# Down projection of a gated MLP in seven block products instead of eight, with the block sums made beside the up projection

## The chip, the cores and the metric

The kernel runs on one core of one Trainium2 chip. The metric is the device time of one execution, in microseconds (us). The core has five engines that run side by side, each through its own list of instructions in order: TensorE (PE, matmuls; PEld is its weight load), VectorE (DVE), ScalarE (ACT), GpSimd (POOL), and SyncE (SP), which here issues all the DMAs. They wait for one another by semaphores. Matmuls write to PSUM, eight banks of 512 float32 for each of 128 partitions; everything else lies in SBUF or in device memory (DRAM).

## The reference, cut to what matters

One encoder layer on a sequence of 1024 positions with 1024 channels, batch 1, all in float32. A mixer of two groups of attention heads comes first and is not touched. The channel half is what the change works on:

```python
h = modulate(rmsnorm(x, g_mlp_norm[l]), sh_m, sc_m)
u = causal_dwconv(jnp.dot(h, w_up[l]), conv_w[l], conv_b[l])      # (1024, 5632)
gate, val = jnp.split(u, 2, axis=-1)
x = x + g_m[:, None, :] * jnp.dot(jax.nn.silu(gate) * val, w_down[l])  # w_down (2816, 1024)
```

`g_m` is a row of 1024 numbers, the last of six slices of `silu(c) @ w_ada + b_ada`; it multiplies the columns of the down product.

## The kernel before, in words

**Precision.** Every large product is made in three matmuls. An operand is split into a high half `hi` (the value as the type fp32r, made by ACT in `hi_of`) and a low half `lo` (the difference, made by POOL or DVE in `lo_of`, line 82), and the product is hi·hi + hi·lo + lo·hi, three matmuls of 128x128 by 128x512 into the same PSUM bank.

**Order.** The program is written with a tile framework. Tiles come from pools, a tag with `bufs=n` has n buffers in turn, and a new tile in a buffer waits for the readers of the old one. A scheduler with a timeline of its own sets the order of the instructions on each engine from the program; `tc.issue_after(x)` makes what is issued under it stand behind instruction x.

**Up phase.** `w_up` (1024 x 5632) is used in 22 tiles j, each with 128 gate and 128 value columns, over 1024 positions. The product of a 2 x 2 block weight (a11, a12, a21, a22, blocks of 512 x 128) with a 2 x 2 block activation is made in seven block products instead of eight, in the manner of Strassen and Winograd: seven sums of weight blocks times seven sums of activation blocks. The activation sums are made and split once ahead of the phase (pages `b11`, `b21`, `t3`, `t2`, `t1`, `t4`, `b22`). In each tile, `ff_head` loads two weight tiles `raw` and makes the products wa·b11 and wb·b21; `ff_tile` makes the weight sums on DVE (lines 1020 to 1035), splits them (ACT and POOL) and makes the products wc·t3, wd·t2, we·t1, wf·t4, wg·b22; each is 4 x 3 = 12 matmuls, so a tile has 84. The products are combined on DVE out of PSUM (lines 1026 to 1037) into c, four blocks of 512: gate and value for 1024 positions. `conv` makes the depthwise convolution (one ACT pass, line 1005, and two DVE passes, 1006 and 1007, for each of gate and value); SiLU (ACT, line 1041) and the product (DVE, line 1042) follow, and the result is stored to `g_d[j]` in DRAM, 128 x 1024.

**Gate row.** From tile 2 on, `gate_row` makes g_m in slices beside the tiles: it loads parts of `w_ada`, adds them up on DVE into `gmbc` (line 993, two passes of 512 in a tile, eight tiles), and two small matmuls bring the sum to all 128 partitions.

**Down phase** (lines 1054 to 1081). The positions are done in two halves h of 512. In each half, all eight PSUM banks hold sums for four position tiles t and two halves n of the output columns. For each of the 22 blocks j of 128 rows, a weight tile 128 x 1024 of `w_down` is loaded, multiplied by `gmbc` (DVE, line 1062) and split (ACT, and POOL for the low halves `wds`), 128 x 512 of `g_d` is loaded and split (ACT, DVE), and 24 matmuls follow (lines 1072 to 1074). Then DVE adds the residual x1 from DRAM (line 1080), and the rows are stored. The weights are loaded and split once in each half.

Of the kernel before, what the change touches and what calls it, by code (L numbers as in the profile page):

```python
# [62 lines left out]
def layer_kernel(ctx, tc, I, out):  # L63
# [3 lines left out]
    def f32(ap):  # L67
        return ap.bitcast(F32)
# [4 lines left out]
    def hi_of(eng, o, i):  # L73
        if eng == "a":
            act.activation(o, i, AF.Copy)  # L75
# [14 lines left out]
    g_d = dram.tile([NF, P, S], F32, name="g_d")  # L90
# [767 lines left out]
    B, v0, hpools = {}, {}, [h2p]  # L858
# [9 lines left out]
    def bpage(nm, k, v, le):  # L868
        pg = hpools[-1].tile([P, 2, 512], F32R, name=f"{nm}_{k}")
        hi_of("a", pg[:, 0], v[:])  # L870
        lo_of(le, pg[:, 1], v[:], pg[:, 0])
        B[nm, k] = pg
# [36 lines left out]
    hpools.append(bp2.__enter__())  # L909
# [15 lines left out]
    def product(pt, w, b):  # L925
        for k in range(4):
            sh, sl = w[:, 0, k * P:(k + 1) * P], w[:, 1, k * P:(k + 1) * P]
            pg = B[b, k]
            pe.matmul(pt, sh, pg[:, 0], start=(k == 0), stop=False)  # L929
            pe.matmul(pt, sh, pg[:, 1], start=False, stop=False)  # L930
            pe.matmul(pt, sl, pg[:, 0], start=False, stop=(k == 3))  # L931

    def ff_head(j, p1, p2):
# [6 lines left out]
        product(p1, split(raw[0][:, :512], f"wa{j}", "w2"), "b11")  # L940
        product(p2[:, :512], split(raw[0][:, 512:], f"wb{j}", "w2"), "b21")
        return raw, p1, p2

    pre = ps2.tile([P, 1024], F32, name="op_0", tag="op", bufs=3)
    head = ff_head(0, pre[:, :512], pre[:, 512:])
    pc = mt("raw", [P, D], "p12_0")
    act.activation(pc[:], pre[:], AF.Copy)
    head = (head[0], pc[:, :512], pc[:, 512:])
# [23 lines left out]
    def bank(tag, name, n=1):  # L972
        return ps3.tile([P, n * 512], F32, name=name, tag=tag, bufs=1)
# [36 lines left out]
    def ff_tile(j, head):  # L1010
        raw, p1, p2 = head
        a11, a12, a21, a22 = raw[0][:, :512], raw[0][:, 512:], raw[1][:, :512], raw[1][:, 512:]
        p5, p6, p34 = bank("p5", f"p5_{j}"), bank("p6", f"p6_{j}"), bank("p34", f"p34_{j}", 2)

        c = mt("c", [P, 7, 512], f"c{j}")
        if j:
            act.activation(c[:, 0], p1, AF.Copy)

        t3 = mt("s", [P, 512], f"ws3_{j}")
        dve.tensor_tensor(t3[:], a11, a21, op=SUB)  # L1020
        p7 = p2[:, 512:] if j else bank("p1", "p7_0")[:]
        product(p7, split(t3[:], f"wc{j}"), "t3")
        dve.tensor_tensor(a21, a21, a22, op=ADD)
        dve.tensor_tensor(a11, a21, a11, op=SUB)
        product(p6[:], split(a11, f"wd_{j}"), "t2")
        dve.tensor_tensor(c[:, 6], c[:, 0] if j else p1, p6[:], op=ADD)
        if j:
            dve.tensor_tensor(c[:, 0::5][:, 0:2], c[:, 0::6][:, 0:2], p2[:].rearrange("p (a b) -> p a b", a=2), op=ADD)
        else:
            dve.tensor_tensor(c[:, 0], p1, p2, op=ADD)  # L1030
            dve.tensor_tensor(c[:, 5], c[:, 6], p7, op=ADD)
        product(p5[:], split(a21, f"we{j}"), "t1")
        dve.tensor_tensor(c[:, 3:5], c[:, 5:7], p5[:].unsqueeze(1).to_broadcast([P, 2, 512]), op=ADD)
        product(p34[:, 512:], split(a22, f"wf{j}"), "t4")
        dve.tensor_tensor(a12, a12, a11, op=SUB)
        product(p34[:, :512], split(a12, f"wg{j}"), "b22")
        dve.tensor_tensor(c[:, 1:3], c[:, 4:6], p34[:].rearrange("p (a b) -> p a b", a=2), op=ADD)  # L1037
# [3 lines left out]
        act.activation(ug[:], ug[:], AF.Silu)  # L1041
        dve.tensor_tensor(ug[:], ug[:], uv[:], op=MUL)
        sp.dma_start(g_d[j], ug[:])

    gr_gen = gate_row()
    for j in range(NF):
        if j:
            head = ff_head(j, bank("p1", f"p1_{j}")[:], bank("p27", f"p27_{j}", 2)[:])
        ff_tile(j, head)
        if j >= 2:  # L1050
            next(gr_gen, None)


    for h in range(2):
        wide = [bank(n, f"dn{n}_{h}", 2) for n in ("p27", "p34")]
        pts = [[w[:, :512], w[:, 512:]] for w in wide]
        for x in (("p1", "p6"), ("p5", "G")):
            pts.append([bank(n, f"dn{n}_{h}")[:] for n in x])
        for j in range(NF):
            raw = mt("raw", [P, D], f"wd{h}_{j}")  # L1060
            sp.dma_start(raw[:], I["w_down"][j * P:(j + 1) * P, :])
            dve.tensor_tensor(raw[:], raw[:], gmbc[:], op=MUL)  # L1062
            w = [split(raw[:, n * 512:(n + 1) * 512], f"wds{h}_{j}{n}") for n in range(2)]
            gr = mt("s", [P, 512], f"gr{h}_{j}")
            sp.dma_start(gr[:], g_d[j][:, h * 512:(h + 1) * 512])
            g = mt("w2", [P, 2, 512], f"g{h}_{j}", F32R)
            hi_of("a", g[:, 0], gr[:])
            lo_of("v", g[:, 1], gr[:], g[:, 0])
            for t in range(4):
                sh, sl = g[:, 0, t * P:(t + 1) * P], g[:, 1, t * P:(t + 1) * P]  # L1070
                for n in range(2):
                    pe.matmul(pts[t][n], sh, w[n][:, 0], start=(j == 0), stop=False)  # L1072
                    pe.matmul(pts[t][n], sh, w[n][:, 1], start=False, stop=False)  # L1073
                    pe.matmul(pts[t][n], sl, w[n][:, 0], start=False, stop=(j == NF - 1))  # L1074
        for t in range(4):
            xt = mt("u", [P, D], f"xo{h}{t}")
            sp.dma_start(xt[:], x1_d[4 * h + t])
            for n in range(2):
                c = slice(n * 512, (n + 1) * 512)
                dve.tensor_tensor(xt[:, c], xt[:, c], pts[t][n], op=ADD)  # L1080
            sp.dma_start(out[(4 * h + t) * P:(4 * h + t + 1) * P, :], xt[:])
# [5 lines left out]
    hpl.__exit__(None, None, None)  # L1087
# [69 lines left out]
```

## Time and profile before

| | us |
|---|---|
| median of 3 runs (1454.95 to 1457.18) | 1456.5 |
| the profiled execution | 1456.2 |
| its span, first to last instruction | 1454.4 |
| PE busy in the span | 1270.4 (87%) |
| DVE busy | 1029.9 (71%) |
| POOL busy | 770.3 (53%) |
| ACT busy | 606.5 (42%) |
| first matmul of tile 0's wc in the up phase | at 770.0 |
| first matmul of the down phase | at 1194.4 |
| last matmul | at 1443.5 |
| granted TensorE clock, mean over the span | 0.936 |

How to read what follows: a row of the timeline is start, duration, engine, line, operation, output<-input, shape, count, and in brackets the idle time ahead of it on its engine with what ended it. A row of waits is the waiting engine and tile, who released it, the total, the number of times and the longest. A row of the groups has the count, then busy time and the mean in ns of one, then the idle time ahead of the group. Matmul durations overlap, since they are pipelined; the distance from one start to the next is what counts. DMA share is the mean busy share of the core's 16 DMA engines.

### The profile page before, as it was taken

Reading aid. Unit: us, or ns where it says so; the run is one execution under the profiler, and the core shown is the slowest. Engines: PE = TensorE matmul, PEld = TensorE weight load, DVE = VectorE, ACT = ScalarE, POOL = GpSimd, SP = SyncE. Lnnn points to the kernel's source line nnn. Section 1 sums busy time; section 2 is a strip of 40 time slices with the busy share of each in tenths; the row PEclk is TensorE's granted clock in tenths of the full one; section 3 lists DMA queues with packets and bytes.
Section 4 is the critical chain, followed back from the end, with each engine's and each line's share of the span. In section 5 each row is a group of like instructions: output and inputs, shape, how many; then the busy total and the mean of one; then the engine's idle time right before and its main releaser. Section 6 shows DMA issues by size and latency. Waiting matters only on the chain.

```text
span 1454.4 us, 20116 instructions
## 1 busy us (share of the span) xinstructions
PE 1270.4 (87%) x6836; PEld 1054.4 (72%) x6836; DVE 1029.9 (71%) x1838; ACT 606.5 (42%) x1182; POOL 770.3 (53%) x717
## 2 busy tenths in 40 slices
PE   3859988998877789886668999999999998999997
PEld 2749877887765568675546877888888887887885
DVE  6964776576688988782577778778777776566653
ACT  4544344334455555452374343443444433322331
POOL 5363544265545764333735655556655555665662
PEclk9979997999887799997878999999999999999999
DMA  7423547555522588778712322322222234447442
GB/s 283 135 70 77 130 107 144 133 119 118 114 59 55 107 162 171 149 145 261 243 41 87 116 88 101 107 82 87 88 87 87 96 130 152 152 142 241 146 145 101
DMA packets 214627, 183.85 MB, mean 126 GB/s; under 512 B 148214, under 2 KB 179066, under 8 KB 213500
## 3 DMA queue, kind: packets, MB, share of 16 engines
q1 hardware_dynamic: 214524, 182.56, 45.3%
q8 instruction: 54, 0.88, 0.3%
q14 instruction: 49, 0.40, 0.1%
HBM read 119.07 MB, written 28.84 MB: 102 GB/s over the span
## 4 chain that ended last, share of the span: by engine, by line
PE 23%; POOL 9%; DVE 8%; issue 8%; DMA 7%; ACT 1%; SPq 1%; DVEq 0%; POOLq 0%; ACTq 0%
PE p L929 5%; PE p L931 5%; PE p L930 5%; POOL wds L82 5%; DMA wu<-w_up 2%; PE dnp L1072 2%; PE dnp L1074 2%; PE dnp L1073 2%; DVE u L1007 1%; DMA wd<-w_down 1%; DVE ws L1020 1%; DVE u L1006 1%; POOL wf L82 1%; POOL we L82 1%; POOL wd L82 1%
## 5 line engine op out<-in xcount | busy, mean ns | idle before, releaser
L82 POOL TENSOR_TENSOR wds<-wd,wds 128x512 fp32r<-128x512 f32 x88 | 152.4, 1753 | 102.7 <-ACT wds L75 102.7
L82 POOL TENSOR_TENSOR wc<-ws,wc 128x512 fp32r<-128x512 f32 x22 | 65.2, 2962 | 136.7 <-ACT wc L75 136.7
L1062 DVE TENSOR_TENSOR wd<-wd,gmbc 128x1024 f32<-128x1024 f32 x44 | 68.5, 1556 | 84.1 <-DMA wd<-w_down 84.0
L1074 PE MATMUL dnp<-wds,g 128*128 128x512 f32 x308 | 119.3, 393 | 4.6 <-DVE g L82 4.6
L1072 PE MATMUL dnp<-wds,g 128*128 128x512 f32 x308 | 120.0, 392 | 1.8 <-DVE xo L1080 1.7
L75 ACT ACTIVATE wds<-wd 128x512 fp32r<-128x512 f32 x88 | 54.8, 624 | 159.1 <-PE dnp L1074 152.3
L1073 PE MATMUL dnp<-wds,g 128*128 128x512 f32 x308 | 120.1, 391 | 0.0
L71 POOL TENSOR_SCALAR hlm<-Pm,rim 128x512 f16<-128x512 f32 (+3 forms) x96 | 64.8, 685 | 78.9 <-DVE rim L684 39.7
L71 POOL TENSOR_SCALAR hlc<-Pc,ric 128x640 f16<-128x640 f32 (+2 forms) x64 | 46.2, 724 | 80.6 <-DVE ric L684 39.5
L1020 DVE TENSOR_TENSOR ws<-wu,wu 128x512 f32<-128x512 f32 x22 | 30.5, 1387 | 75.0 <-DMA wu<-w_up 75.0
L681 ACT ACTIVATE Pc<-sc,mc 128x640 f32<-128x640 f32 (+2 forms) x64 | 42.2, 660 | 91.0 <-DVE mc L670 64.1
L655 PE MATMUL sm<-mk,mq 96*128 96x512 f32 (+3 forms) x288 | 71.2, 377 | 10.2 <-ACT Pm L681 6.7
L1006 DVE SCALAR_TENSOR_TENSOR u<-c,pk,u 128x1023 f32<-128x1023 f32 x44 | 77.4, 1766 | 1.8 <-ACT u L1005 1.8
L1041 ACT ACTIVATE u<-u 128x1024 f32<-128x1024 f32 x22 | 23.4, 1063 | 132.1 <-DVE u L1007 132.1
L655 PE MATMUL sc<-k,q 64*128 64x512 f32 (+3 forms) x288 | 68.7, 365 | 10.7 <-ACT Pc L681 6.8
L82 DVE TENSOR_TENSOR g<-gr,g 128x512 fp32r<-128x512 f32 x44 | 69.8, 1588 | 11.2 <-ACT g L75 11.2
L430 DVE SCALAR_TENSOR_TENSOR aacc<-aw,cs,aacc 128x256 f32<-128x256 f32 x84 | 44.1, 525 | 47.3 <-DMA aw<-w_ada 47.0
L1005 ACT ACTIVATE u<-c,pk 128x1024 f32<-128x1024 f32 x44 | 52.3, 1236 | 56.1 <-DVE c L1037 56.1
L705 DVE SCALAR_TENSOR_TENSOR hlm<-Pm,rim,hlm 128x512 f16<-128x512 f32 (+3 forms) x96 | 68.5, 727 | 6.1 <-POOL hlm L71 5.9
L721 PE MATMUL pvm<-PTm,vt 128*128 128x128 f16 x576 | 47.2, 232 | 28.6 <-DMA PTm<-hlm 24.5
L1074 PEld LDWEIGHTS dnp<-wds,g 128*128 128x128 f32 x308 | 58.2, 189 | 18.0 <-DVE g L82 5.9
L1072 PEld LDWEIGHTS dnp<-wds,g 128*128 128x128 f32 x308 | 58.1, 189 | 15.1 <-DVE xo L1080 2.6
(366 smaller groups left out, 4281.1 us busy)
## 6 DMA issues: line engine op xcount, KB each, us to landing
wu<-w_up SPq DMA_DIRECT2D x44, 512.0 KB, 4.5
wd<-w_down SPq DMA_DIRECT2D x44, 512.0 KB, 5.1
aw<-w_ada SPq DMA_DIRECT2D x96, 128.0 KB, 2.4
g_d<-u SPq DMA_DIRECT2D x22, 512.0 KB, 2.6
gr<-g_d SPq DMA_DIRECT2D x44, 256.0 KB, 3.6
x<-x SPq DMA_DIRECT2D x16, 512.0 KB, 6.6
adaw<-w_ada_a SPq DMA_DIRECT2D x8, 1024.0 KB, 5.2
wq_r<-w_qk SPq DMA_DIRECT2D x32, 128.0 KB, 2.8
```

The source lines that it names most:

```text
L71: pool.tensor_scalar(o, i, s, 1.0, op0=MUL, op1=MUL)
L82: (pool if eng == "p" else dve).tensor_tensor(o, i, f32(hi), op=SUB)
L655: last = pe.matmul(s[:, c:c + w], qpg[rs_, a, q], kpgs[kh][rs_, b, ko:ko + w], start=(a == 0 and b == 0), stop=(a == 1))
L705: dve.scalar_tensor_tensor(hl[:, w:2 * w], pp, ri[:], hl[:, :w], op0=MUL, op1=SUB)
L929: pe.matmul(pt, sh, pg[:, 0], start=(k == 0), stop=False)
L930: pe.matmul(pt, sh, pg[:, 1], start=False, stop=False)
L931: pe.matmul(pt, sl, pg[:, 0], start=False, stop=(k == 3))
L1006: dve.scalar_tensor_tensor(u[:, 1:], c[:, :S - 1], pk[:, cv + 1:cv + 2], u[:, 1:], op0=MUL, op1=ADD)
L1062: dve.tensor_tensor(raw[:], raw[:], gmbc[:], op=MUL)
L1072: pe.matmul(pts[t][n], sh, w[n][:, 0], start=(j == 0), stop=False)
L1073: pe.matmul(pts[t][n], sh, w[n][:, 1], start=False, stop=False)
L1074: pe.matmul(pts[t][n], sl, w[n][:, 0], start=False, stop=(j == NF - 1))
```

## The change

The down product is now also made in seven block products. The 22 row blocks of `w_down` are taken in 11 pairs i (block 2i and 2i+1), the output columns in two halves, the positions in two halves, so that for each i there is a 2 x 2 block of weights (each 128 x 512) and a 2 x 2 block of activations (each 128 x 512). A stage is one of the seven products, summed over all 11 pairs in PSUM: 11 x 4 position tiles x 3 matmuls, in four banks. The stages P1, P2, P5, P6, P3, P7, P4 take two sets of four banks (A and B) in turn; P3 and P7 are added onto what P5 and P6 left in their banks.

- **Activation sums.** They are made on DVE in the up phase, at the end of a tile: one difference of 512 columns for even j, three sums for odd j. `g_d` now holds seven blocks for each pair, and `keep` stores them: 256 KiB twice for even j, 512 KiB twice and 256 KiB once for odd j. Down stages load one block of 256 KiB for each i.
- **Weight sums.** The four weight blocks of a pair are loaded once and stay in the tile `R[i]` (5 x 512; the fifth part is the activation). DVE makes the sums in place, in the stage before they are needed (`extra`).
- **Splits** in the down stages take weight and activation in one pass, 128 x 1024: ACT the high half, DVE the low half (`halves`); POOL has no part in the stages. The splits have four buffers, and a fifth now and then.
- **Early part.** In the last up tile, `early` loads and splits the first four pairs for stage P1.
- **Gate row at the output.** `gmbc` multiplies the output blocks instead of the weights. Output blocks are combined in SBUF (`p1s`, `w5`, `u2`), two position tiles at a time (128 x 1024), by items of `todo` put between the low halves from the sixth pair of a stage on; x1 is added to them. The last four blocks are multiplied, added and stored 512 columns at a time, and P4 does its last three pairs position tile by position tile (`group=3`).
- **Order.** `inorder` keeps DVE passes and SP loads of the stages in the program's order.
- **Up phase.** The PSUM tag p27 is gone: wb·b21 is added onto wa·b11 in the same bank, and ACT copies that bank twice. p1 has two banks, and `wa` and the weight sums of the next tile are issued ahead of `wg` of this one. Buffers: raw 4 for 3, s 7 for 5, u 3 for 2; c has 4 blocks for 7.

In PE's order the first product of tile 1 (wa·b11) stands ahead of tile 0's wc; before, nothing stood there. The diff, cut:

```diff
-    g_d = dram.tile([NF, P, S], F32, name="g_d")
+    g_d = dram.tile([7, NF // 2, P, 512], F32, name="g_d")
...
-    MB = {"raw": 3, "w2": 2, "s": 5, "ws": 5, "c": 2, "u": 2}
+    MB = {"raw": 4, "w2": 2, "s": 7, "ws": 5, "c": 2, "u": 3}
...
+    def halves(src, nm):
+        w = sptile(nm)
+        hi_of("a", w[:, 0], src)
+        if "dl" in E:
+            tt(w[:, 1], src, f32(w[:, 0]), SUB)
+        else:
+            lo_of("v", w[:, 1], src, w[:, 0])
+        return w
...
+    def early():
+        hpl.__exit__(None, None, None)
...
+        for i in range(4):
+            r = mt("raw", [P, D], f"de{i}").rearrange("p (a b) -> p a b", a=2)
+            sp.dma_start(r[:, 0], wsrc(i, 0))
+            sp.dma_start(r[:, 1], g_d[A_G11, i])
+            dq[i] = halves(r, f"dne{i}")
...
+        if j:
+            with tc.issue_after(p3_last[0]):
+                product(p1[:], wb, "b21", add=True)
+            act.activation(c[:, 0], p1[:], AF.Copy)
+            if j == NF - 1:
+                early()
...
+        product(p34[:, 512:], wf, "t4")
+        if j + 1 < NF:
+            raw, wa, wb = ff_load(j + 1)
+            q1 = bank("p1", f"p1_{j + 1}")
+            product(q1[:], wa, "b11")
+            d = mt("c", [P, 4, 512], f"c{j + 1}")
+            act.activation(d[:, 3], q1[:], AF.Copy)
+            nxt = ff_sums(j + 1, raw) + [wb, q1, d]
+        p3_last[0] = product(p34[:, :512], wg, "b22")
...
-        sp.dma_start(g_d[j], ug[:])
+        i = j // 2
+        lo, hi = ug[:, :512], ug[:, 512:]
+        sm = mt("s", [P, 512], f"gs{j}")
+        if j % 2 == 0:
+            us.append(ug)
+            keep(0, 1, i, lo)
+            dve.tensor_tensor(sm[:], lo, hi, op=SUB)
+            keep(6, 1, i, sm[:])
+        else:
+            ue = us.pop()
+            keep(1, 2, i, ug[:])
+            dve.tensor_tensor(ue[:, 512:], ue[:, 512:], hi, op=ADD)
+            dve.tensor_tensor(ue[:, :512], ue[:, 512:], ue[:, :512], op=SUB)
+            keep(3, 2, i, ue[:])
+            dve.tensor_tensor(sm[:], lo, ue[:, :512], op=SUB)
+            keep(5, 1, i, sm[:])
...
-            dve.tensor_tensor(raw[:], raw[:], gmbc[:], op=MUL)
-            w = [split(raw[:, n * 512:(n + 1) * 512], f"wds{h}_{j}{n}") for n in range(2)]
...
+    def stage(nm, bk, b, kind, add=False, wq=None, extra=None, todo=(), group=0):
...
+        for i in range(NK):
+            if wq is not None and not (nm == "P1" and i in dq):
+                wload(i, wq[0], wq[1])
+            if nm == "P2" and i in dq:
+                wload(i, 0, 0)
+            if nm == "P1" and i in dq:
+                w = dq[i]
+            else:
+                gload(i, kind)
+                w = halves(R[i][:, b::4 - b], f"dn{nm}_{i}")
+            if extra is not None:
+                extra(i)
+            if i < NK - group:
+                for t in range(4):
+                    mm3(bk, t, w, i == 0 and not add, i == NK - 1, add)
+            else:
+                held.append((i, w))
+            if i >= 5:
+                for _ in range(-(-len(todo) // (NK - i))):
+                    todo.pop(0)()
...
+    stage("P1", "A", 0, A_G11, wq=(0, 0))
+    stage("P2", "B", 1, A_G12, wq=(1, 2), todo=[copy_p1],
+          extra=lambda i: (wload(i, 2, 1), tt(R[i][:, 0], R[i][:, 2], R[i][:, 0], SUB)))
+    stage("P5", "A", 0, A_S1, todo=c11(),
+          extra=lambda i: (wload(i, 3, 3), tt(R[i][:, 0], R[i][:, 3], R[i][:, 0], SUB)))
+    stage("P6", "B", 0, A_S2, todo=[ext(wq_, p1s, "A", x) for x in range(2)],
+          extra=lambda i: tt(R[i][:, 2], R[i][:, 3], R[i][:, 2], SUB))
+    stage("P3", "A", 3, A_S4, add=True, todo=[ext(u2, p1s, "B", x) for x in range(2)],
+          extra=lambda i: tt(R[i][:, 1], R[i][:, 1], R[i][:, 0], SUB))
+    stage("P7", "B", 2, A_S3, add=True, todo=after(u2, u2, "A", 0, 1))
...
+    stage("P4", "A", 1, A_G22, todo=[ext(wq_, wq_, "B", 0), ext(wq_, wq_, "B", 1), ext(p1s, p1s, "B", 0), ext(p1s, p1s, "B", 1)]
+          + after(wq_, wq_, "B", 1, 1)[2:] + pre_, group=3)
+    for t in range(4):
+        o = dl.tile([P, 512], F32, name=f"oe{t}", tag="oe", bufs=3)
+        tt(o[:], banks[f"A{t // 2}"][:, t % 2], gmbc[:, :512], MUL)
+        tt(o[:], o[:], p1s[:, t], ADD)
+        sp.dma_start(out[(4 + t) * P:(5 + t) * P, :512], o[:])
```

More of the change, by code (lines that the diff above doesn't have):

```diff
@@ L923, in split, with product @@
         return w
-    def product(pt, w, b):
+    def product(pt, w, b, add=False):
         for k in range(4):
@@ L928, in product, with ff_load @@
             pg = B[b, k]
[L929 to L933, printed above, removed]
+            pe.matmul(pt, sh, pg[:, 0], start=(k == 0 and not add), stop=False, skip_group_check=add)
+            pe.matmul(pt, sh, pg[:, 1], start=False, stop=False, skip_group_check=add)
+            last = pe.matmul(pt, sl, pg[:, 0], start=False, stop=(k == 3), skip_group_check=add)
+        return last.ins
+    def ff_load(j):
         raw = []
@@ L1045, in layer_kernel @@
+        return nxt
     gr_gen = gate_row()
+    p3_last = [None]
+    cur = ff_sums(0, raw0) + [None, None, mt("c", [P, 4, 512], "c0")]
     for j in range(NF):
[L1047 to L1049 removed]
+        cur = ff_tile(j, cur)
         if j >= 2:
             next(gr_gen, None)
[L1054 to L1061, printed above, removed]
[L1062 to L1081 removed]
@@ new lines, in layer_kernel, with inorder, two @@
+    R[:3] = [dl.tile([P, 5, 512], F32, name=f"dnr{i}") for i in range(3)]
+    tail = {}
+    def inorder(eng, f, *a, **k):
+        if eng in tail:
+            with tc.issue_after(tail[eng]):
+                r = f(*a, **k)
+        else:
+            r = f(*a, **k)
+        tail[eng] = r.ins
+    banks = {}
+    for n in ("B0", "B1", "A0", "A1"):
+        banks[n] = None
+    def two(n, name):
+        banks[n] = ps4.tile([P, 2, 512], F32, name=name, tag=n, bufs=1)
+    for n in ("B0", "B1", "A0", "A1"):
+        two(n, f"dn{n}_0")
@@ new lines, in rows, with finish_out, mul, add @@
+    def rows(t0, n, d):
+        return d[t0:t0 + 2, :, n * 512:(n + 1) * 512].rearrange("t p c -> p t c")
+    out_v = out.rearrange("(t p) c -> t p c", p=P)
+    def finish_out(h, n, x, src, o, store=True):
+        t0 = 4 * h + 2 * x
+        xt = []
+        def mul():
+            xt.append(pair(f"xo{h}{n}{x}"))
+            load(xt[0][:], rows(t0, n, x1_d))
+            tt(o, src, gm_of(n), MUL)
+        def add():
+            tt(o, o, xt[0][:], ADD)
+            if store:
+                sp.dma_start(rows(t0, n, out_v), o)
+        return [mul, add]
```

156 lines of the change are left out of this document (122 added, 34 removed).

## The prediction

> **What bounds the kernel now.** I read the page first: span, engine shares, costliest groups.
>
> ```profile
> span 1454.4 us, 20116 instructions
> PE 1270.4 (87%) x6836; PEld 1054.4 (72%) x6836; DVE 1029.9 (71%) x1838; ACT 606.5 (42%) x1182; POOL 770.3 (53%) x717
> ```
>
> The profiled execution took 1456.2 us, 1.8 outside its span, and stands 0.3 below the median of 1456.5; sums below are against 1456.2. Then stages: a table of stretches (us; busy time of PE, PEld, DVE, ACT, POOL; granted clock; DMA share; GB/s). The first row is the up phase without gate-row work, the second with it, the third the down projection, the last two the densest loading.
>
> ```profile
> 1060.00:1155.00 95.00, 95.00 (x421) 78.65 (x420) 73.39 (x67) 40.06 (x55) 54.47 (x36) 1.00 0.25 84
> 866.75:946.65 79.90, 77.24 (x337) 62.77 (x337) 62.81 (x61) 31.16 (x44) 46.34 (x29) 1.00 0.30 106
> 1195.00:1444.00 249.00, 242.45 (x1055) 198.15 (x1053) 148.19 (x101) 77.25 (x129) 145.56 (x85) 0.99 0.46 152
> 0.00:20.00 20.00, 3.58 (x8) 1.45 (x8) 6.70 (x13) 11.48 (x21) 10.04 (x25) 1.00 0.90 340
> 1320.00:1340.00 20.00, 17.62 (x74) 13.30 (x73) 11.25 (x9) 5.23 (x9) 9.46 (x6) 1.00 0.83 288
> ```
>
> PE is never idle in the first row. Since a busy PE need not be PE at its peak, I took start to start from the timeline: the first matmul of two following tiles, the gap ahead of the first tile, a pair of slow starts after it, and the first and last matmul of the down projection.
>
> ```profile
> 1085.63 0.39 PE L929 MATMUL p<-t,wc 128*128 128x512 f32 x1
> 1104.67 0.39 PE L929 MATMUL p<-t,wc 128*128 128x512 f32 x1
> 770.04 0.80 PE L929 MATMUL p<-t,wc 128*128 128x512 f32 x1 [14.11 <-ACT wc L75]
> 773.10 0.63 PE L931 MATMUL p<-t,wc 128*128 128x512 f32 x1
> 773.52 0.63 PE L929 MATMUL p<-t,wc 128*128 128x512 f32 x1
> 1194.43 0.39 PE L1072 MATMUL dnp<-wds,g 128*128 128x512 f32 x1
> 1443.46 0.39 PE L1074 MATMUL dnG<-wds,g 128*128 128x512 f32 x1
> ```
>
> 84 matmuls in 19.04 us are 0.2267 us each, so both MLP phases are bound by their number of matmuls. The down projection has 2 halves x 22 x 4 x 2 x 3 = 1056; its 1055 steps need 239.1 us and took 249.0: 9.9 us are stalls. PE's waits, the first two rows in the up phase, the others in the down projection:
>
> ```profile
> PE p L929 <- ACT wc L75: 14.1, 1, 14.1
> PE p L929 <- DVE c L1028: 4.5, 6, 0.9
> PE dnp L1074 <- DVE g L82: 4.6, 3, 2.0
> PE dnp L1072 <- DVE xo L1080: 1.7, 2, 1.1
> ```
>
> The rest of the 9.9 are slow starts after such waits, like the 0.43 us step above.
>
> **The change, part by part.**
>
> *Matmuls.* Seven stages x 11 x 4 x 3 = 924 for 1056: 132 x 0.2267 = **-29.9 us**. The Trainium skill ("TensorE: Matmul & The Clock Gate", Back-to-back issue gap) gives N/2.4 + 2.5 ns for a lone matmul and about 131 ns sustained at N=512; by these the term would be 28.5 or 17.3 us (estimates from that page). The trace's 0.2267 us on fp32r fits neither, and decides.
>
> *Feeding the seven stages.* A step is 12 matmuls, 2.72 us. ACT makes one 128x1024 high half, DVE one low half; POOL does nothing. Rows for such passes, and spacings on DVE and POOL:
>
> ```profile
> L1041 ACT ACTIVATE u<-u 128x1024 f32<-128x1024 f32 x5 | 5.3, 1063 | 29.1 <-DVE u L1007 29.1
> L1005 ACT ACTIVATE u<-c,pk 128x1024 f32<-128x1024 f32 x10 | 11.9, 1236 | 3.6 <-DVE c L1037 3.6
> 1112.37 0.68 DVE L1024 TENSOR_TENSOR wu<-wu,wu 128x512 f32<-128x512 f32 x1
> 1112.98 1.21 DVE L1042 TENSOR_TENSOR u<-u,u 128x1024 f32<-128x1024 f32 x1
> 1114.11 0.68 DVE L1035 TENSOR_TENSOR wu<-wu 128x512 f32<-128x512 f32 x1
> 1114.71 0.67 DVE L1026 TENSOR_TENSOR c<-c,p 128x512 f32<-128x512 f32 x1
> 1115.42 1.22 DVE L1028 TENSOR_TENSOR c<-c,p 128x1024 f32<-128x1024 f32 x1
> 1113.01 2.94 POOL L82 TENSOR_TENSOR wc<-ws,wc 128x512 fp32r<-128x512 f32 x1 [5.83 <-ACT wc L75]
> 1115.90 1.30 POOL L82 TENSOR_TENSOR wd<-wu,wd 128x512 fp32r<-128x512 f32 x1
> 1117.16 1.30 POOL L82 TENSOR_TENSOR we<-wu,we 128x512 fp32r<-128x512 f32 x1
> ```
>
> ACT: 1.06 of 2.72, hidden. DVE: 1.21 for the low half, 0.68 for the weight-block sum that four stages (P2, P5, P6, P3) make for the next. The fullest stage is P5 with six 128x1024 output passes: 11 x 1.89 + 6 x 1.21 = 28.1 of 29.9 us. Hidden, but barely; the cover is four or five split buffers, about 8 us of lead. P4 has twelve output passes, two between each of its last low halves, and the first waits for P7's last matmul. Its sixth low half gets a buffer when the stage's second step ends (5.4), is done at 6.6, and five more rounds of 3 x 1.21 end at 24.8; the grouped last three blocks want it at 8 steps + 6 matmuls = 23.1. Cost between 0 and 5; I take **+2**.
>
> *The old stalls* come from the half change (xo) and the starved start (g); the new stages alternate two sets of four banks, so the next starts in banks read long before. **-9.9**, or 0 if as much returns. At the entry four blocks (10.9 us of PE) are split inside the last tile. Behind it DVE has one 1.22 add, then waits for ACT's first conv pass (1.24), has four conv passes of 1.2 and the first low half: about 9 us. Held, with 2 us to spare.
>
> *Loads.* 121 of 256 KiB, eight of x1, 4.2 MB out: 40 MB, 192 GB/s over the stages where the trace shows 152. P2 is the worst: 37 loads, 9.4 MB after the first, on SP behind the last tile's stores at about 16 us into the stages (three stores follow DVE's interleaved sums), due by 54.6: 243 GB/s. The rows with 340 and 288 show that the engines can; 0, up to +8 if not.
>
> *Tail.*
>
> ```profile
> 1447.70 1.28 DVE L1080 TENSOR_TENSOR xo<-xo,dnp 128x512 f32<-128x512 f32 x2 [5.25 <-DMA xo<-x_d]
> 1449.02 2.10 SPq L1081 DMA_DIRECT2D out_dram<-xo  x2
> 1450.07 0.68 DVE L1080 TENSOR_TENSOR xo<-xo,dnG 128x512 f32<-128x512 f32 x1
> ```
>
> Before, 10.9 us pass from the last matmul to the end: residual tiles wait for a buffer. After, x1 is added beforehand, and the last 512 columns take a multiply and an add: 0.4 + 2 x 0.68, then the store, 3.3 us as now (1451.1 to 1454.4): 5.1. **-5.8.** The gate row multiplied 44 weight tiles on DVE; at the output it is eight passes and four short ones, counted above.
>
> *Up phase, first product.* The next tile's first product now stands ahead of wc in PE's order and needs only ready pages, so 12 matmuls run inside the 14.1 us gap: **-2.7**. Its two splits add 1.25 us to ACT in a stretch where DVE sets the pace; 0 to +1.3, I take 0.
>
> *Up phase, VectorE.* Every second tile adds one 512-wide difference, the others three; the p27 eviction (1.22) becomes 0.61. ACT copies one more bank (half of the 1.06 above, against 42% busy); stores go from 22 to 55 DMAs against a DMA share of 0.25; SP loads weights two tiles ahead instead of one, which removes DVE's wait for them. The p27 bank and its 4.5 us of waits are gone. What could take its place: wc above started beside L1042, had to let L1042 and L1035 through and ran 1.24 us beside L1026, which reads PSUM. So passes with two SBUF inputs and POOL's take turns. Gate-row rows:
>
> ```profile
> 857.43 1.27 DVE L1006 SCALAR_TENSOR_TENSOR u<-c,pk,u 128x1023 f32<-128x1023 f32 x1
> 858.63 0.74 DVE L993 SCALAR_TENSOR_TENSOR gmbc<-adaw,cs,gmbc 128x512 f32<-128x512 f32 x1
> 859.29 1.27 DVE L1007 SCALAR_TENSOR_TENSOR u<-c,pk,u 128x1022 f32<-128x1022 f32 x1
> ```
>
> Turns per tile: four sums 2.4, four conv passes 4.8, L1042 1.1, seven POOL splits at 1.26, 8.8: 17.2 of 19.04. The sums add 0.6 or 1.8, giving 17.8 and 19.0; the gate row adds 2 x 0.66: 19.7 in the mean, 0.7 too much in eight tiles. That is 5.4 us for the 4.5 that go: **0**, between -4.5 and +8.
>
> That is also a rule of the Trainium skill ("SBUF — State Buffer", Who interferes with whom): a VectorE instruction with two SBUF inputs and a GpSimd one that reads SBUF hold the shared port in turn, one fully blocking. The trace agrees (2.94 us for 1.30).
>
> Sum: -29.9 + 2 - 9.9 - 5.8 - 2.7 = -46.3; 1456.2 - 46.3 = **1410 us**.
>
> **The rivals.**
>
> *The turns decide the up phase.* For it: 19.0 of 19.04 in every second tile, before any latency; DVE also waits 1.2 us for ACT at each tile's start. If that time is not used by POOL, such a tile takes 20.2: 11 x 1.2 + 8 x 0.7 more, less the 5 already granted, about +14: 1424 us. Against: PSUM passes (3.6 us a tile) run beside POOL, and ACT and SP now prepare earlier. The SBUF rule named above is this rival's mechanism.
>
> *The stalls only move.* The matmuls go, but entry, P2, P5 or P4 starve as the old loop did, each followed by a slow start: 9.9 back and a fuller P4, 1410 + 10 + 3 = 1423. For it: margins of 2 us at the entry and in P5. Against: buffers four deep.
>
> *The loads bound the stages: slower.* At 152 GB/s, the rate of the old stage, the 38 MB after the entry last 250 us for 211: 1449. The sign turns at 147 GB/s (258 us, 1457); 140 gives 1470. For it: 512-column pieces are half as long as the old weight rows, one SP queue issues all in order, and a blocked store holds loads. Against: 152 used a share of 0.46.
>
> *It does nothing.* The stages last as long as the old loop; 1450 to 1459. Only with the loads at just under 152.
>
> **How the numbers follow.** Forecast 0.70, turns 0.12, moved stalls 0.10, loads below 147 0.05, nothing 0.01, other slow ends 0.02. Likeliest: 1410. Downwards all taken costs vanish: P4's 2 and the 4.5 of waits, 1403, and 2 more for a shorter store: 1401. Upwards 1424 plus the 8 of P2: 1432. Chances of faster, within 0.2% (what a measurement of this kernel can tell from no change) and slower: 0.92, 0.01, 0.07.
>
> **What would show it.** Right: 924 down matmuls at 0.227 us; stage P1 begins within 1 us of the last up matmul, near 1192; last matmul near 1403 and 5 us behind it; gaps of 1 to 2 us late in P4 alone; tiles of 19.04 us outside the gate row. Wrong: PE waiting on POOL for wc in every second tile (turns); gaps behind DVE low halves in P5 or ACT waiting for DMA on dnr in P2 (moved stalls, loads); any PE clock below 1.0 in the stages, which nothing here prices.

## The result, and the profile after

The changed kernel took 1435.5 us (median of 4 runs, 1430.8 to 1436.8) against 1455.7 us for the kernel before in the same session: a ratio of 0.986, with a 95% interval of 0.983 to 0.988. The forecast was 1410 us in a range of 1401 to 1432. The kernel became faster, by 20 us for the 46 foretold, and its time lies above the range.

The profiled execution took 1436.0 us. Its page, first two lines of numbers and the shares of the chain that ended last:

```profile
span 1434.2 us, 19853 instructions
PE 1248.0 (87%) x6704; PEld 1029.5 (72%) x6704; DVE 1100.8 (77%) x1935; ACT 619.9 (43%) x1150; POOL 628.6 (44%) x629
DVE 23%; PE 19%; issue 6%; ACT 4%; DMA 3%; POOL 2%; SPq 1%; POOLq 0%; DVEq 0%; ACTq 0%
```

The same line of the page before:

```profile
PE 23%; POOL 9%; DVE 8%; issue 8%; DMA 7%; ACT 1%; SPq 1%; DVEq 0%; POOLq 0%; ACTq 0%
```

VectorE has moved from third to first place in the chain. The stretches of the profile after (columns as in the prediction): the up phase without and with the gate row, the whole down phase, and stage P2 within it.

```profile
1060.00:1155.00 95.00, 92.11 (x399) 74.25 (x398) 81.44 (x69) 41.35 (x61) 57.76 (x34) 1.00 0.28 94
866.75:946.65 79.90, 73.58 (x311) 57.43 (x311) 70.76 (x60) 32.93 (x48) 46.49 (x28) 1.00 0.35 113
1218.00:1428.00 210.00, 209.57 (x925) 173.17 (x923) 161.25 (x162) 82.56 (x78) 0.00 (x0) 1.00 0.56 191
1245.00:1275.00 30.00, 30.00 (x134) 24.86 (x133) 23.65 (x27) 15.62 (x15) 0.00 (x0) 1.00 1.05 386
```

In 95 us without the gate row PE now makes 399 matmuls where it made 421. The timeline has the matmuls that mark the phases: first matmul of wc in tiles 0, 1 and 2, in two later tiles, and the first and last of the down phase.

```profile
773.23 0.79 PE L932 MATMUL p<-t,wc 128*128 128x512 f32 x1 [10.62 <-ACT wc L75]
792.40 0.39 PE L932 MATMUL p<-t,wc 128*128 128x512 f32 x1
808.73 0.39 PE L932 MATMUL p<-t,wc 128*128 128x512 f32 x1
1160.33 0.50 PE L932 MATMUL p<-t,wc 128*128 128x512 f32 x1
1180.96 0.39 PE L932 MATMUL p<-t,wc 128*128 128x512 f32 x1
1217.84 0.39 PE L1171 MATMUL dnA<-dne 128*128 128x512 f32 x1
1427.79 0.39 PE L1173 MATMUL dnA_P<-dnP 128*128 128x512 f32 x1
```

With the rows of before, the spans split up so (us):

| | before | after | difference | foretold |
|---|---|---|---|---|
| start to wc of tile 0 | 770.0 | 773.2 | +3.2 | 0 |
| up phase, from there to the first down matmul | 424.4 | 444.6 | +20.2 | -2.7 |
| first to last down matmul | 249.0 | 210.0 | -39.1 | -37.8 |
| last matmul to the end | 11.0 | 6.4 | -4.6 | -5.8 |

The first row varies by as much between runs of other kernels below (767.1 to 773.5), so I put nothing on it. Of the 26.0 us between the profiled execution and the forecast, 22.9 lie in the up phase. In tiles 14 to 20, where no gate row is at work, before had 19.04 us in each; after they are 19.94, 20.06, 20.47, 20.63, 19.49, 20.63 and 19.50 (from start to start of wc), a mean of 20.1, which makes 7.4 us. The larger part lies beside the gate row: tiles 4 to 13 took 198.2 us before and 212.9 after, 14.7 more. The experiments below look at the tiles without the gate row, since it doesn't mix in there; a tile time without further word is the mean of tiles 15 to 20.

The waits that say who is late in the up phase are VectorE's own. In the same stretch, 960 to 1180 us: before, then after (fences hold one row each).

```profile
DVE ws L1020 <- DMA wu<-w_up: 41.2, 11, 4.2
```

```profile
DVE u L1023 <- ACT u L1022: 23.4, 11, 3.0
```

Before, VectorE waited for loads, and PE was busy throughout the stretch without the gate row. After, it waits only for ScalarE's first conv pass, once in each tile (lines 1022 to 1024 are the conv of the kernel after: ScalarE's pass and VectorE's two); and PE waits for what comes out of VectorE's queue through ScalarE and GpSimd (775 to 1190 us, the three largest of five rows, which add up to 19.0 us):

```profile
PE p L934 <- POOL wc L82: 8.3, 11, 1.2
PE p L932 <- ACT wc L75: 4.8, 7, 1.1
PE p L932 <- ACT c L1092: 3.6, 4, 1.3
```

One tile on VectorE and GpSimd, from the timeline of after. L949, 951, 952 and 956 are the four weight sums of the next tile, L1095 the last pass out of PSUM, L1107 to L1115 the block sums, L1100 the product with SiLU.

```profile
1118.12 0.69 DVE L1115 TENSOR_TENSOR gs<-u,u 128x512 f32<-128x512 f32 x1
1118.73 0.69 DVE L949 TENSOR_TENSOR ws<-wu,wu 128x512 f32<-128x512 f32 x1
...
1121.04 1.57 DVE L956 TENSOR_TENSOR wu<-wu 128x512 f32<-128x512 f32 x1
1122.54 1.21 DVE L1095 TENSOR_TENSOR c<-c,p 128x1024 f32<-128x1024 f32 x1
1125.39 4.20 DVE L1023 SCALAR_TENSOR_TENSOR u<-c,pk,u 128x1023 f32<-128x1023 f32 x2 [1.65 <-ACT u L1022]
1129.51 4.54 DVE L1024 SCALAR_TENSOR_TENSOR u<-c,pk,u 128x1022 f32<-128x1022 f32 x2
...
1126.23 2.27 POOL L82 TENSOR_TENSOR wa<-wu,wa 128x512 fp32r<-128x512 f32 x1
1128.47 2.26 POOL L82 TENSOR_TENSOR wg<-wu,wg 128x512 fp32r<-128x512 f32 x1
1130.70 2.27 POOL L82 TENSOR_TENSOR wb<-wu,wb 128x512 fp32r<-128x512 f32 x1
```

Four conv passes last 8.7 us here where 4.8 would do alone: they alternate with GpSimd's splits of wa, wg and wb. And the sum for the next wc (L949) has its place behind the block sums, right before the tile that needs it: the first matmul of that wc starts at 1120.21, 1.5 us later. In the kernel before, the timeline has the next L1020 (the same sum) a tile early, ahead of the conv passes and 19.5 us ahead of the wc that it is for:

```profile
1104.25 1.78 DVE L1020 TENSOR_TENSOR ws<-wu,wu 128x512 f32<-128x512 f32 x1 [3.60 <-DMA wu<-w_up]
1105.96 2.30 DVE L1006 SCALAR_TENSOR_TENSOR u<-c,pk,u 128x1023 f32<-128x1023 f32 x1
...
1123.71 0.39 PE L929 MATMUL p<-t,wc 128*128 128x512 f32 x1
```

### The profile page after: what moved, and what is told of

Read it like the earlier page. It is cut to its first block, busy times and chain, and to the rows that moved or that the text cites. A ratio compares the mean times of both kernels' runs of the same rounds, so it can differ in the third digit from the quotient of the medians.

```text
span 1434.2 us, 19853 instructions
## 1 busy us (share of the span) xinstructions
PE 1248.0 (87%) x6704; PEld 1029.5 (72%) x6704; DVE 1100.8 (77%) x1935; ACT 619.9 (43%) x1150; POOL 628.6 (44%) x629
## 4 chain that ended last, share of the span: by engine, by line
DVE 23%; PE 19%; issue 6%; ACT 4%; DMA 3%; POOL 2%; SPq 1%; POOLq 0%; DVEq 0%; ACTq 0%
DVE u L1024 6%; DVE u L1023 4%; PE dnA_P L1171 2%; PE dnA_P L1172 2%; PE dnA_P L1173 2%; ACT u L1022 2%; DVE u L1100 2%; PE dnB_P L1171 1%; PE dnB_P L1172 1%; PE dnB_P L1173 1%; DVE wu L951 1%; DVE c L1095 1%; DMA adaw<-w_ada 1%; DVE wu L952 1%; DVE c L1085 1%
## 5 line engine op out<-in xcount | busy, mean ns | idle before, releaser
L75 ACT ACTIVATE dnP<-dnr 128x1024 fp32r<-128x1024 f32 x73 | 77.4, 1061 | 109.9 <-PE dnA_P L1173 46.4
L1145 DVE TENSOR_TENSOR dnP<-dnr,dnP 128x1024 fp32r<-128x1024 f32 x72 | 88.0, 1224 | 44.2 <-ACT dnP L75 44.1
L82 POOL TENSOR_TENSOR wc<-ws,wc 128x512 fp32r<-128x512 f32 x22 | 32.3, 1466 | 169.4 <-ACT wc L75 169.4
L1024 DVE SCALAR_TENSOR_TENSOR u<-c,pk,u 128x1022 f32<-128x1022 f32 x44 | 88.5, 2050 | 0.0
L721 PEld LDWEIGHTS <-vt 128*128 128x128 f16 x576 | 39.8, 106 | 40.4 <-issue 38.7
L681 ACT ACTIVATE Pm<-sm,mm 128x128 f32<-128x128 f32 (+3 forms) x64 | 47.2, 737 | 46.1 <-DVE mm L674 30.1
L655 PEld LDWEIGHTS sm<-mk,mq 96*128 96x128 f32 x288 | 50.5, 204 | 20.4 <-ACT Pm L681 10.2
L655 PEld LDWEIGHTS sc<-k,q 64*128 64x128 f32 x288 | 46.4, 202 | 23.0 <-ACT Pc L681 8.8
L150 PE MATMUL ipq<-wq_s,hT 128*128 128x256 f32 x192 | 56.7, 295 | 0.0
L151 PE MATMUL ipq<-wq_s,hT 128*128 128x256 f32 x192 | 55.2, 288 | 0.0
L705 DVE SCALAR_TENSOR_TENSOR hlc<-Pc,ric,hlc 128x640 f16<-128x640 f32 (+2 forms) x64 | 48.3, 760 | 8.2 <-POOL hlc L71 8.1
```

Of the source, the lines that this page charges most:

```text
L150: pe.matmul(pt, sh, mh, start=(start and i == 0), stop=False)
L151: pe.matmul(pt, sh, ml, start=False, stop=False)
L655: last = pe.matmul(s[:, c:c + w], qpg[rs_, a, q], kpgs[kh][rs_, b, ko:ko + w], start=(a == 0 and b == 0), stop=(a == 1))
L681: act.activation(pr[:, :n], sv, AF.Exp, bias=m[:], scale=-1.0, accum_out=rsum[:, 0:1])
L705: dve.scalar_tensor_tensor(hl[:, w:2 * w], pp, ri[:], hl[:, :w], op0=MUL, op1=SUB)
L721: last = pe.matmul(u.pv[:, c], u.vst(j), mov, start=(x == 0), stop=(x == len(todo) - 1))
```

## The experiments

Two theories stood at first. **A**: VectorE's and GpSimd's turns at their shared port fill the tile, as the first rival said. **B**: the place of the sums in VectorE's queue delays the next wc. A third (**C**) was formed after the first four runs. Times are medians; ratios are to the kernel before in the same session, with 95% intervals.

**No block sums.** `keep` stores other blocks in their place; the VectorE passes are gone.

```diff
-            dve.tensor_tensor(sm[:], lo, hi, op=SUB)
-            keep(6, 1, i, sm[:])
+            keep(6, 1, i, hi)
```

(and so the three of an odd tile.)

> The changed kernel without the activation sums: VectorE makes none of the four differences and sums per pair of tiles; the stages load unsummed blocks of the same size, so every DMA, split and matmul stays (the output is not the layer's). Theory A (turns): VectorE passes with two SBUF inputs and GpSimd's splits hold a port in turn, and the 1.2 us of sums a tile push that total too near the tile's 19.04 us of matmuls. Theory B (place in the queue): the sums stand ahead of the next tile's weight sums on VectorE, so wc is late; the port plays no part. Both: tiles go back to 19.0 to 19.3 us outside the gate row, stages begin near 1195 to 1198, time 1410 to 1416. If tiles stay at 20 us, the sums are not the cause at all and the new order of the up phase is.

Measured: 1421.7 us, 0.977 (0.975 to 0.980); the up phase 429.7 us, tiles without the gate row 19.04. The sums are worth 14 us of the whole, 14.9 of the 22.9 in the up phase. But the run isn't a clean removal: its trace has L949 between the conv passes (at 1098.44, behind three of the four), so the scheduler also set another order when the sums went.

**Block sums on GpSimd.**

```diff
-            dve.tensor_tensor(sm[:], lo, hi, op=SUB)
+            pool.tensor_tensor(sm[:], lo, hi, op=SUB)
```

(and so the other three.)

> The activation sums are made by GpSimd for VectorE; all else as in the changed kernel. Theory A: the same work holds the port for 1.26 us instead of 0.6 us for each 512 columns, 1.3 us a tile more turns: tiles of 20.5 to 22 us, 1445 to 1470. Theory B: VectorE's queue is free of the sums, tiles of 19.0 to 19.4 us, 1412 to 1420.

Measured: 1424.1 us, 0.979 (0.977 to 0.981). It fits neither: the tiles are at B's edge, the time above B's range. GpSimd has more to do at the port, and yet the kernel gains 11 us; but VectorE, freed of 1.4 us a tile, does not reach 19.04 (19.4). A full port alone and a full queue alone are both too simple.

**Low halves of wa and wb on VectorE** (in the up phase).

```diff
-        lo_of("p", w[:, 1], src, w[:, 0])
+        lo_of("v" if nm[:2] in ("wa", "wb") else "p", w[:, 1], src, w[:, 0])
```

> The low halves of wa and wb are made by VectorE for GpSimd in the up phase; all else as in the changed kernel. Theory A: each holds the port for 0.6 us instead of 1.26, 1.3 us a tile less turns, and two of the splits that ran into the conv passes are gone: tiles of 19.0 to 19.4 us, stages begin near 1197, 1412 to 1420. Theory B: VectorE has 1.2 us a tile more ahead of the weight sums: tiles of 20.5 to 21.5 us, 1445 to 1460.

Measured: 1413.7 us, 0.972 (0.969 to 0.975), tiles of 19.15 without the gate row. A's numbers fit. VectorE has two passes more in each tile and the kernel is 22 us faster, so the number of passes in its queue is not the cause. Nor is the late place of the weight sums by itself: they still stand right before their tile (L949 at 1116.20, the first matmul of its wc at 1121.78). B as it stood falls. VectorE's groups, 960 to 1180 us, for after and then for this run:

```profile
L1024 DVE SCALAR_TENSOR_TENSOR u<-c,pk,u 128x1022 f32<-128x1022 f32 x22 | 46.9, 2168 | 0.0
L1023 DVE SCALAR_TENSOR_TENSOR u<-c,pk,u 128x1023 f32<-128x1023 f32 x22 | 41.4, 1920 | 23.4 <-ACT u L1022 23.4
```

```profile
L1023 DVE SCALAR_TENSOR_TENSOR u<-c,pk,u 128x1023 f32<-128x1023 f32 x22 | 34.3, 1599 | 10.7 <-ACT u L1022 10.7
L1024 DVE SCALAR_TENSOR_TENSOR u<-c,pk,u 128x1022 f32<-128x1022 f32 x22 | 27.2, 1274 | 0.0
```

The conv passes fall from 88.3 to 61.5 us in eleven tiles, 2.4 us a tile, for the two low halves taken on (about 0.7 us each where nothing else ran). What cost was that GpSimd's splits ran beside the conv passes; two of the three are gone here.

**Sums alone in the kernel before**, stored as a tile of their own.

```diff
+    g2_d = dram.tile([NF, P, 512], F32, name="g2_d")
...
         sp.dma_start(g_d[j], ug[:])
+        sm = mt("s", [P, 512], f"gs{j}")
+        for _ in range(1 if j % 2 == 0 else 3):
+            dve.tensor_tensor(sm[:], ug[:, :512], ug[:, 512:], op=SUB)
+        sp.dma_start(g2_d[j], sm[:])
```

> The kernel before with differences of the same size and number added on VectorE in the up phase (one of 512 columns in even tiles, three in odd ones, and one store of 256 KiB a tile); their results are not used, the output is the layer's. Theory A: turns per tile go from 17.2 to 18.4 us of 19.04, as in the changed kernel; the tiles should lengthen to 19.5 to 20.5 us, +8 to +20, 1465 to 1478. Theory B: the old order has the next tile's first weight sum ahead of the conv passes, a tile early; the sums cost under 5 us, 1455 to 1461.

Measured: 1666.3 us, 1.146 (1.143 to 1.149), tiles of 28.4 us. This answers another question than the one asked. The waits of SP's queue and of PE:

```profile
SPq L1044 <- DVE u L1043: 371.8, 21, 20.2
...
PE p L930 <- ACT wc L75: 138.1, 21, 8.2
```

SP stands 18 us a tile at the store of u, waiting for VectorE, with the next `w_up` loads behind it. In the kernel before it stands there too, 11.5 us a tile (230.0 in 20 waits), while PE is busy throughout (95.00 of 95 us). The added tile and store had changed two orders: on SP each pair of loads stands one store of u later, and on VectorE the sum for wc now stands behind the conv passes, right before its tile (L1021 at 1086.13, wc at 1087.59). Which of the two costs the 9 us a tile was not tried.

**Theory C**, formed from these: in the order that the kernel after has, VectorE itself is the bound. Its passes, the stretches that splits take from it and the wait for ScalarE come to 20 us in a tile, and the next wc hangs at the end. The next run brings VectorE's queue near the order that the kernel before had, with everything left in.

**Block sums a tile later**, behind the next tile's L1095 (`pend` holds them back; the store of u stays where it was).

```diff
+        c3 = dve.tensor_tensor(c[:, 1:3], c[:, 1:3], p34[:]..., op=ADD)
+        if pend:
+            with tc.issue_after(c3.ins):
+                pend.pop()()
...
+        if j < NF - 2:
+            pend.append(sums)
+        else:
+            sums()
```

> The changed kernel with the block sums of a tile issued a tile later, behind the next tile's last PSUM pass (L1095 of the kernel after) and so beside ScalarE's first conv pass, where VectorE stood idle 23.4 us in eleven tiles. This puts VectorE's queue in the order of the kernel before: the next weights' first sum ahead of the conv passes, a tile early. Nothing is added or left out, and GpSimd keeps all low halves. Theory C (VectorE's in-order chain is the bound: its own passes, the stretches in which a GpSimd split holds the shared port, and the idle time for ScalarE add up to 20.06 us, and the next tile's wc hangs at the end): filling the 2.1 us of idle time brings tiles without the gate row to 19.04 to 19.3 us and the whole to 1416 to 1425. Theory A (turns at the shared port set the time, wherever the passes stand): these tiles stay at 19.9 to 20.3 us, the whole at 1430 to 1440.

Measured: 1411.4 us, 0.971 (0.969 to 0.974), better than expected by C. Tiles without the gate row are 19.04 to the hundredth, and tiles 4 to 13, beside the gate row, take 200.9 us for the 212.9 of after. VectorE's waits in the stretch from 960 to 1180 us, and its timeline in one tile:

```profile
DVE c L1095 <- PE p L934: 22.3, 10, 2.9
```

```profile
1082.59 1.22 DVE L1095 TENSOR_TENSOR c<-c,p 128x1024 f32<-128x1024 f32 x1 [2.47 <-PE p L934]
1083.72 1.41 DVE L1112 TENSOR_TENSOR gs<-u 128x512 f32<-128x512 f32 x1
1085.06 0.68 DVE L949 TENSOR_TENSOR ws<-wu,wu 128x512 f32<-128x512 f32 x1
1085.77 0.69 DVE L951 TENSOR_TENSOR wu<-wu 128x512 f32<-128x512 f32 x1
1086.38 1.28 DVE L1023 SCALAR_TENSOR_TENSOR u<-c,pk,u 128x1023 f32<-128x1023 f32 x1
1087.58 0.69 DVE L952 TENSOR_TENSOR wu<-wu,wu 128x512 f32<-128x512 f32 x1
1088.18 1.28 DVE L1023 SCALAR_TENSOR_TENSOR u<-c,pk,u 128x1023 f32<-128x1023 f32 x1
1089.37 4.55 DVE L1024 SCALAR_TENSOR_TENSOR u<-c,pk,u 128x1022 f32<-128x1022 f32 x2
```

VectorE now waits for PE (and once, 0.9 us, for a load of the gate row): it runs ahead, and PE is the bound again. The weight sums stand among the conv passes, a tile early, and two of the conv passes fall into GpSimd's idle time (1.28 us each). Collisions remain (4.55 us for two passes, splits of 2.27), with 16.8 us of VectorE and 12.3 of GpSimd busy in each tile of 19.04, and cost nothing: against A, a busy port is no bound by itself.

**Late sums and the low halves together.**

> As the run before it, and with the low halves of wa and wb on VectorE instead of GpSimd. Theory C: both reliefs act on the same chain, so all tiles without the gate row at 19.04 us and the rest of the gate row's tiles nearer to 20.0: 1404 to 1412, under the 1413.7 of the low halves alone. Theory A: the order adds nothing to the low halves, 1411 to 1416.

Measured: 1411.2 us, 0.971 (0.968 to 0.973): the same as the late sums alone, since PE is the bound already. That lies in both expected ranges, so the run doesn't part the theories. Its up phase is 421.2 us, as the prediction had it (421.7).

**Low halves of wa, wb and wg on VectorE.**

> The changed kernel with the low halves of wa, wb and wg on VectorE (wa and wb alone gave 1413.7). Each takes 0.68 us of VectorE and takes one 1.26 us split off the shared port. Theory C: VectorE's own work grows to some 17.2 us in a tile, one collision less, idle time unchanged: within 4 us of 1413.7. Theory A: better again by 4 to 8 us, 1405 to 1410.

Measured: 1412.3 us, 0.972 (0.969 to 0.974): as C said, and short of A's 1405 to 1410. Its tiles without the gate row are 19.04, PE's own time, so there was little left to gain by either.

**Which part of the late order helps?** In the late sums two things moved: the sums fill the time in which VectorE waited for ScalarE, and the weight sums came early. This run keeps the first and holds the second back, with two `issue_after` (the weight sums behind L1085, L1095 behind the last weight sum), so that VectorE's order is that of after except for the block sums.

```diff
+            with tc.issue_after(c2.ins):
+                nxt = ff_sums(j + 1, raw) + [wb, q1, d]
...
+        with tc.issue_after(w4[0]):
+            c3 = dve.tensor_tensor(c[:, 1:3], c[:, 1:3], p34[:]..., op=ADD)
```

> The block sums moved behind the next tile's last PSUM pass as in the run of the late sums, but with the rest of VectorE's queue held in the order of the kernel after: the four weight sums stand together between L1085 and L1095, ahead of the conv passes, and no first weight sum comes a tile early. Theory C1 (what the sums cost is the idle time for ScalarE that they now fill): tiles without the gate row 19.04 to 19.3 us, the whole 1411 to 1420. Theory C2 (what helped was the next tile's wc a tile early): these tiles 19.7 to 20.2 us, the whole 1425 to 1437.

Measured: 1439.4 us, 0.990 (0.988 to 0.991), tiles of 20.08. Theory C1 falls; C2's tiles fit, and the whole is 2 us above its range. The idle time was filled, 4.9 us for the 23.4 of after (960 to 1180 us):

```profile
DVE u L1025 <- ACT u L1024: 4.9, 4, 1.8
```

And the tile got no shorter: VectorE's busy time went from 17.6 to 18.9 us a tile, because what moved up met GpSimd's splits (the block sums take 28.0 us in this stretch where the kernel after has 14.3 for as many). The 28 us between this run and the late sums come from the two `issue_after`, that is from the place of the weight sums and of the splits that follow them. The reverse, early weight sums with the block sums at the tile's end, was not tried.

**Three raw buffers.** The late sums with `"raw": 3`.

> The kernel with late sums, with three raw buffers as the kernel before has, not four. If the kernel before left no room for the sums because its next load starts only when GpSimd's last split frees a buffer, and VectorE then waits for it (39.2 us in eleven tiles of the kernel before with sums): VectorE waits for w_up again, 2 to 4 us in a tile, tiles of 19.6 to 21 us, the whole 1422 to 1445. If that wait was only spare time: 1411 to 1414, tiles 19.04 us.

Measured: 1416.8 us, 0.973 (0.970 to 0.976), between the two expectations. Tiles without the gate row stay at 19.04, so the fourth buffer isn't what keeps loads out of the way. Of the 3.6 us more in the up phase 2.7 are one tile: the second takes 19.04 us again and not 16.3, so the first product no longer ran ahead.

**Sums alone in the kernel before, without a new tile or store**: into a dead block of c.

```diff
         sp.dma_start(g_d[j], ug[:])
+        for _ in range(1 if j % 2 == 0 else 3):
+            dve.tensor_tensor(c[:, 5], ug[:, :512], ug[:, 512:], op=SUB)
```

> The kernel before with the same number of 128x512 VectorE passes as the block sums added to its up phase (one or three in turn, 2.07 us for a pair's tile on average 1.38 us, two passes), written into a dead block of c and used by nothing, so without a new tile or store: what is computed and stored is as before. Theory C: that kernel's order has the next tile's wc ready a tile early and VectorE has 14.9 us in a tile of 19.04: no change, 1454 to 1460. Theory A: the added passes collide too: tiles of 19.6 to 20.2 us, 1464 to 1475.

Measured: 1476.5 us, 1.016 (1.012 to 1.019), tiles of 19.67. C expected no change, and misses; A's tiles fit, and the whole is 1.5 us above its range. VectorE had 4.2 us of idle time in each tile of the kernel before, but to passes at this place it was of no use. The rows that show it, from this run's timeline, and then GpSimd's split of wc in its groups (2955 ns for one before, same stretch):

```profile
1080.73 1.82 DVE L1020 TENSOR_TENSOR ws<-wu,wu 128x512 f32<-128x512 f32 x1 [3.57 <-DMA wu<-w_up]
1100.49 1.31 DVE L1020 TENSOR_TENSOR ws<-wu,wu 128x512 f32<-128x512 f32 x1 [4.09 <-DMA wu<-w_up]
...
1089.52 3.54 POOL L82 TENSOR_TENSOR wc<-ws,wc 128x512 fp32r<-128x512 f32 x1 [5.83 <-ACT wc L75]
```

```profile
L82 POOL TENSOR_TENSOR wc<-ws,wc 128x512 fp32r<-128x512 f32 x11 | 36.8, 3350 | 53.3 <-ACT wc L75 53.3
```

As I read the rows, the tile is a closed ring: VectorE's conv passes, SiLU and the split of wc behind it on ScalarE, GpSimd's splits, which free the raw buffers, the load, and VectorE's next L1020, which waits for it. The sums aren't in the ring, but stand beside the split of wc and hold it up, by 0.4 us in the mean, where a tile is 0.6 longer. The links of the ring were not tried one by one; the next run tries the place of the sums.

**The same sums a tile later**, behind L1037, where VectorE waits for that load.

> The kernel before with the same added VectorE passes as in the run e8 (one or three in turn, into a dead block of c, used by nothing), but a tile later, behind its last PSUM pass (the first two of them beside the load that VectorE waits for there, 39.2 us in eleven tiles), where GpSimd is ending its splits, not beside GpSimd's split of wc. Theory P (what a VectorE pass costs here depends on what it stands beside: in e8 the sums held up GpSimd's splits, which free the buffer for the next load, and VectorE's wait for that load closes the ring): tiles without the gate row 19.04 to 19.2 us, the whole 1453 to 1461. Theory N (the count of passes sets it, in this kernel as in the changed one): tiles of 19.6 us, the whole 1468 to 1478 as in e8.

Measured: 1460.8 us, 1.005 (1.003 to 1.006), tiles without the gate row 19.04. The same passes cost 7 us there, not 23, and VectorE's wait for loads shrank:

```profile
DVE ws L1020 <- DMA wu<-w_up: 12.4, 11, 1.7
```

Theory P holds. What is placed in the wait itself did find room, then: VectorE is busy 18.0 us in each tile of 19.04.

## Why the prediction was wrong

**Up phase, VectorE (0, between -4.5 and +8): measured +22.9.** This is the step that failed, and the only one that matters. It added up the turns at the port over a tile, got 17.8 and 19.0 of 19.04 us (19.7 with the gate row), and called the sums hidden. Three things were missing.

- *The order within VectorE's queue.* The kernel before had the next tile's first weight sum a tile early. I took the new order as earlier all round ("ACT and SP now prepare earlier"); in the trace, wc's sum had gone to the end of the queue, right before its use. With the early order put back the up phase took 424.8 us (late sums) and 421.2 (with the low halves moved too), against 421.7 foretold, and the kernel 1411.4 and 1411.2 against 1410.
- *Waits in series.* A sum of turns has no room for a wait. The 1.2 us for ScalarE at the tile's head stood in the rival and measured 2.1 (23.4 in eleven tiles). VectorE runs in order, so this adds to its passes: 17.6 busy, 2.2 waiting (both in tiles 15 to 20), and small gaps make the 20.1 us. That the wait costs anything by itself isn't shown: with most of it filled, the tile stayed at 20.08.
- *Collisions depend on place.* The same port rule that the prediction named ("SBUF — State Buffer", Who interferes with whom, in the Trainium skill) holds in the trace: two conv passes beside GpSimd's splits last 4.54 us, where 2.4 would do alone. But how often the two engines meet is set by the order: with the same passes and splits VectorE was busy 16.8 us a tile (late sums), 17.6 (after) and 18.9 (late sums, weight sums held together).

The rival "the turns decide the up phase" (1424) was the right direction and the right place, with a chance of 0.12 that was too small, and 11 us too fast. It had only every second tile late; all of tiles 14 to 20 are. Its mechanism was half of it: fewer splits on GpSimd do cure the changed kernel (1413.7), but so does another order with all splits left there.

**Matmuls (-29.9) and old stalls (-9.9): right.** The 923 steps from the first down matmul to the last took 210.0 us, 0.2275 us each. The Trainium skill's sustained figure for N=512 ("TensorE: Matmul & The Clock Gate", Back-to-back issue gap), about 131 ns, is again not what this loop on fp32r shows.

**P4 (+2): it did not occur.** PE's waits in the whole down phase of after are one row:

```profile
PE dnA L1172 <- DVE dnP L1147: 0.4, 1, 0.4
```

This one wait is the entry, which was to have 2 us to spare:

```profile
1229.77 0.50 PE L1172 MATMUL dnA<-dnP 128*128 128x512 f32 x1 [0.43 <-DVE dnP L1147]
```

VectorE's first low half of the stage ends at 1229.72, 11.9 us behind the first down matmul and not about 9: VectorE still had passes of the last two tiles to make. P5 and P4 show no wait.

**Loads (0): right.** P2 needed 243 GB/s by the prediction; the row of that stage above shows 386, and PE busy throughout.

**First product (-2.7): right**, as the distance from tile 1 to tile 2 shows, 808.73 - 792.40 = 16.33 us, 72 matmuls.

**Tail (-5.8): measured -4.6.** Two passes were to follow the last matmul; there are four. VectorE's first and last of them, and the one that it waited for, from the timeline:

```profile
1425.72 0.69 DVE L1145 TENSOR_TENSOR oe<-dnA_P,gmbc 128x512 f32<-128x512 f32 x1 [2.61 <-PE dnA_P L1173]
...
1428.39 0.68 DVE L1145 TENSOR_TENSOR oe<-dnA_P,gmbc 128x512 f32<-128x512 f32 x1
...
1430.43 0.69 DVE L1145 TENSOR_TENSOR oe<-oe,p1s 128x512 f32<-128x512 f32 x1
```

Eight passes run without a gap from 1425.7 on, so each output block is a block late; two passes more are 1.3 us, and 5.1 + 1.3 is the 6.4 measured. What kept the first one waiting until then was not tried.

## What to carry to other kernels

When work is added to an engine that runs in order, don't set busy times against the length of a loop: write down the ring that closes the loop, with its waits, and ask what the added work stands beside. The idle time of an engine is spare for a pass only where the pass itself runs in it and holds up nothing of that ring. VectorE's wait for PE had room (late sums). Its wait for a load had room for passes put right into it (7 us for the kernel), and none for the same passes beside the split of wc (23 us). Its wait for ScalarE was filled and nothing gained, since the passes met the splits there. And when the order is a scheduler's, compare the order on each engine before and after; here it was worth 28 us, more than the 14 that came from leaving the sums out.

## What the runs showed of the hardware

- A VectorE pass of 1.20 us and a GpSimd split of 1.26 us, from start to start alone, that alternate take 2.24 us for the pair (splits at 1126.23, 1128.47 and 1130.70), less than their sum of 2.46: about 0.2 us of each pair overlaps. A sum of turns is a little too high.
- The collision goes both ways. In the kernel before the largest loss is GpSimd's (wc 2.96 us in the mean for 1.30 alone); in the kernel after both lose (conv passes of 1.92 and 2.17 us in the mean for 1.28, splits of wa, wg and wb of 2.1 to 2.2 for 1.3).
- A long wait in SP's queue says little by itself: 230.0 us at the store of u in the kernel before, where PE was busy throughout (95.00 of 95 us without the gate row), and 371.8 in the run with an added store, which was 211 us slower. How much of the 211 the queue made is open, since VectorE's order had changed as well.
